# Weight splits moved around a step's events, with a shorter layer-norm chain and fp32 broadcasts, in a two-layer hybrid diffusion backbone

## The chip, the core and the metric

The kernel runs on one core of one Trainium2 chip. TensorE (PE in the rows, PEld for its weight loads) multiplies; VectorE (DVE), ScalarE (ACT) and GpSimd (POOL) do the element-wise work; SyncE (SP) issues the transfers. The metric is the device time of one execution in microseconds, lower is better.

## The reference

Two groups of tokens share the weights: 128 prompt tokens and 256 sample tokens of width 1024, so 384 columns in all. Each of two layers does

```
x <- LN(alpha*x + 0.5*gate1*SwiGLU_1(mod1(x)))
x <- LN(alpha*x + gate2*Mixer(mod2(x)))
x <- LN(alpha*x + 0.5*gate3*SwiGLU_2(mod3(x)))
```

where LN is a layer norm over the 1024 features, mod_i(x) = x*(1+scale_i)+shift_i with scale, shift and gate from a matrix `w_mod` times the conditioning vector, and SwiGLU goes through 2 x 2816 columns. The mixer has one input projection into queries, keys, values, a convolution branch (31 taps per channel), a pooling branch and three gates; differential attention over 4 heads; a projection of each branch, the gated sum of the three, and one output projection. Outputs are both groups' tokens, and keys and values of the prompt. All data is float32.

## The kernel before

Activations lie feature-major: `X` is 8 tiles of 128 features x 384 tokens. Every large matmul is done three times to keep float32 accuracy: weights and activations are split into a high part (`wh`, `xh`: a copy rounded to the matmul's reduced fp32) and a low part (`wl`, `xl`: the rest), and `mm3` adds wh·xh, wl·xh and wh·xl (lines 404, 405, 406) in one PSUM bank.

Weights come as 388 units of 128 x 1024, in the order of use. For each unit SP loads `raw` (8 buffers), ScalarE copies `wh <- raw` (`prep_h`, line 342), VectorE subtracts `wl <- raw - wh` (`prep_l`, line 351). Five buffers hold split units; more lie in the general slots while `extra` allows. One step is one call of `begin`: it makes sure that the units up to `self.lead` ahead are split, runs the step's events, and returns the unit on which TensorE then does 24 matmuls. `lead` starts at 2 behind each layer norm and grows by 1 a step to 5 (9 with `extra`). Events are closures due at a step: evacuations of PSUM banks, the stages of attention (`a`, `b_`, `c`, `d`: scores, softmax, transpose, product with V), the convolution's layer norm, the pooling chain (`low`, `pmm`). Behind the events come `after` work (`fold_tile`, lines 656 and 658), background work (`tap`, the convolution's taps, line 1096) and `mod_dve_step`, which does two multiply-and-sum instructions of 128 x 1024 (line 451) whenever `mod_acc`, raised by `mod_rate` a step, reaches 1. Each engine takes its instructions in the order in which this code issues them.

Six sub-layers s = 0 to 5 run; s = 1 and 4 are the mixers. Each ends in `ln_end`: sums of y and y² by matmuls with ones (`ln_stat`, line 543), a chain of small VectorE instructions on 128 x 3 numbers (lines 728 to 734 with `rsqrt`, three Newton steps), and a broadcast of 1/sigma and -mean/sigma over the partitions by matmuls (line 745). The next sub-layer's first four units are multiplied meanwhile with `X` not yet normalized (lines 699 to 702), and corrected later (`unfold`). The four units are split ahead of it: in the mixer by the steps of `w_out`, whose steps (`self.early`) run the events first and split behind them, copy and subtraction together.

Of the kernel before, what the change touches and what calls it, by code (L numbers as in the profile page):

```python
# [11 lines left out]
F32 = mybir.dt.float32  # L12
F32R = mybir.dt.float32r
BF16 = mybir.dt.bfloat16
I32 = mybir.dt.int32
AF = mybir.ActivationFunctionType
ALU = mybir.AluOpType
AX = mybir.AxisListType

D = 1024  # L20
# [82 lines left out]
NORM_AT = 3  # L103
EXTRA = 4
KIN = 2
RATES = (0.9, 0, 0.65, 0.65, 0, 0.3)

# [133 lines left out]
class Kernel:  # L243
# [5 lines left out]
    def __init__(self, tc, ctx, io):  # L249
        self.tc, self.nc, self.io = tc, tc.nc, io  # L250
        self.pool = ctx.enter_context(tc.tile_pool(name="sb", bufs=1))
        self.ps = ctx.enter_context(tc.tile_pool(name="ps", bufs=1, space=bass.MemoryType.PSUM))
        self.uid = 0
        self.early = False
        self.half = None
        self.cur = 0
        self.n_dma = 0
        self.n_prep = 0
        self.raw = {}
        self.w = {}  # L260
        self.events = []
        self.step = 0
        self.bg = deque()
        self.bg_rate = 0
        self.jobs_done = set()
        self.job_dma = deque()
        self.mv = {}
        self.mod_acc = 0.0
        self.mod_rate = 0.0
        q = [(0, j) for j in range(16, 24)]  # L270
        for i in range(1, 6):
            q += [(i, j) for j in range(24)]
        self.lead = self.NW
        self.extra = self.held = 0
        self.after = []
        self.after_rate = 2
        self.jobs = deque(q)
# [6 lines left out]
    def t(self, shape, dt=F32, name="k"):  # L284
        n = self.nm(name)
        return self.pool.tile(shape, dt, name=n, tag=n, bufs=1)
# [8 lines left out]
        return self.pool.tile([128, 432], F32, name=self.nm(name), tag="c", bufs=8)  # L295

    def tiny(self, n, dt=F32, name="y"):
        return self.pool.tile([128, 16], dt, name=self.nm(name), tag="tiny", bufs=24)[:, :n]

    def bank(self, name="mm"):  # L300
        return self.ps.tile([128, 512], F32, name=self.nm(name), tag="mm", bufs=6)
# [19 lines left out]
            self.n_dma += 1  # L321

    def prep(self, upto):
        while self.n_prep < min(upto, len(UNITS)):
            self.prep_h()
            self.prep_l()

    def prep_h(self):
        u = self.n_prep
        slots = sum(not isinstance(w[0], SlotUnit) for w in self.w.values()) >= self.NW - self.held  # L330
        self.n_prep += 1
        self.dma_w(u + 1)
        cols = UNITS[u][1]
        r = self.raw.pop(u)
        if slots:
            w = tuple(SlotUnit([self.slot(F32R, n) for _ in range(3)]) for n in ("wh", "wl"))
        else:
            w = tuple(self.pool.tile([128, 1024], F32R, name=self.nm(n), tag=n, bufs=self.NW) for n in ("wh", "wl"))
        step = NT if slots else cols
        cuts = [slice(a, min(a + step, cols)) for a in range(0, cols, step)]  # L340
        for c in cuts:
            self.nc.scalar.copy(w[0][:, c], r[:, c])  # L342
        self.w[u] = w
        self.half = (u, r, cuts)

    def prep_l(self):
        u, r, cuts = self.half
        self.half = None
        wh, wl = self.w[u]
        for c in cuts:  # L350
            self.nc.vector.tensor_sub(wl[:, c], r[:, c], wh[:, c].bitcast(F32))  # L351
# [20 lines left out]
    def begin(self, key, run=True):  # L372
        u = self.cur
        assert UNITS[u][0] == key, (UNITS[u][0], key)
        self.step += 1
        if self.early:
            self.run_events()
        self.prep(u + self.lead)
        self.run_events()
        self.lead = min(self.lead + 1, self.NW + self.extra)  # L380
        for _ in range(self.after_rate):
            self.run_after()
        self.dma_w(u + self.NW + self.WDMA)
        for _ in range(self.bg_rate):
            if self.bg:
                self.bg.popleft()()
        self.mod_acc += self.mod_rate
        while self.mod_acc >= 1.0:
            self.mod_acc -= 1.0
            self.mod_dve_step()  # L390
        self.cur += 1
        return self.w.pop(u)
# [268 lines left out]
    def unfold(self, p):  # L661
# [9 lines left out]
        nc.vector.tensor_add(z, z, T)  # L671
        return z

    def ln_end(self, b7, ab, keys):

        nc, st = self.nc, self.lns
# [45 lines left out]
        else:  # L722
            b = self.ln_stat(y7, sq)
            tot = self.tiny(6)
            nc.vector.tensor_add(tot, st["pre"], b[:, :6])
        ms, msq, v = self.tiny(3), self.tiny(3), self.tiny(3)
        rm, rh, rl = self.tiny(6), self.tiny(6, F32R), self.tiny(6, F32R)
        nc.vector.tensor_scalar(ms, tot[:, 0:3], 1.0 / D, None, ALU.mult)
        nc.vector.tensor_tensor(msq, ms, ms, ALU.mult)
        nc.vector.scalar_tensor_tensor(v, tot[:, 3:6], 1.0 / D, msq, ALU.mult, ALU.subtract)  # L730
        self.rsqrt(v, 3, out=rm[:, 0:3])
        nc.vector.scalar_tensor_tensor(rm[:, 3:6], ms, -1.0, rm[:, 0:3], ALU.mult, ALU.mult)
        nc.vector.tensor_copy(rh, rm)
        nc.vector.tensor_sub(rl, rm, rh.bitcast(F32))
        if keys:
            if self.half:
                self.prep_l()
# [1 line left out]
                self.run_after()  # L739
            main(ma, 3)  # L740
        R, M = self.sbank(), self.sbank()
        for o, B in ((0, R), (3, M)):
            for t in range(3):
                for n, x in enumerate((rh, rl)):
                    mm(B[:, 128 * t:128 * t + 128], x[:, o + t:o + t + 1].to_broadcast([128, 128]),
                       self.identr, start=n == 0, stop=n == 1)
        if keys:
            Rs = self.slot(name="R")
            nc.scalar.copy(Rs, R[:, :NT])
# [88 lines left out]
    def ffn(self, l, j, xs, outs, s, mod_rate):  # L838
        nc = self.nc
        self.mod_rate = mod_rate  # L840
        ah = [None] * NF

        def evac(f, g, u, folded=False):
            if folded:
                g, u = self.unfold(g), self.unfold(u)
            sl = self.slot(name="si")
            nc.scalar.activation(sl, g[:, :NT], AF.Silu)
            a = self.slot(name="a")
            nc.vector.tensor_mul(a, u[:, :NT], sl)  # L849

            def split():
                h, lo = self.slot(F32R, "ah"), self.slot(F32R, "al")
                nc.scalar.copy(h, a)  # L853
                nc.vector.tensor_sub(lo, a, h.bitcast(F32))
                ah[f] = (h, lo)
            self.at(1, split)

        if xs is None:
            outs = self.first_group(l, j)
            self.mod_acc = -1.0  # L860
            xs = self.first_xs
        self.ln_begin(s)
        fo = s > 0
        f0 = 3
        if fo:
            o2 = self.kouter([("ffn_in", l, j, 2), ("ffn_in", l, j, NF + 2)], xs, 8, KIN)
            self.at(1, lambda: evac(0, outs[0], outs[1], fo))
            self.at(2, lambda: evac(1, outs[2], outs[3], fo))
            self.at(2, lambda: evac(2, o2[0], o2[1]))
        else:  # L870
            for f in range(3):
                self.at(1, lambda f=f: evac(f, *outs[2 * f:2 * f + 2]))
        for f in range(f0, NF):
            bs = outs[6:] if f == 3 and not fo else []
            if f == 7:
                self.extra = 0
            for c in (f, NF + f)[len(bs):]:
                w = self.begin(("ffn_in", l, j, c))
                b = self.bank()
                self.mtile(b[:, :NT], w, xs)  # L880
                bs.append(b)
            self.at(1, lambda f=f, bs=bs: evac(f, *bs))
        del xs
        for m in range(8):
            b = None
            for q in range(3):
                w = self.begin(("ffn_out", l, j, m, q))
                if m == 0 and q == 2:
                    self.ln_gate()
                    self.ab = None if s == 5 else self.coef_ss(s + 1)  # L890
                if b is None:
                    b = self.bank()
                if m == 5 and q == 0:
                    self.mod_rate = 0
                self.mtile(b[:, :NT], w, ah, 8 * q, 8 if q < 2 else 6, q == 0, q == 2)
            if m < 7:
                self.at(1, lambda m=m, b=b: self.ln_evac(m, b))
        self.flush()
        return b


    def start(self):
# [7 lines left out]
        self.scT = self.scz[:, :, 0:2]  # L910
        self.sel = self.C[:, C_SEL:C_SEL + 2]
        self.ones = self.t([128, 1], name="ones")
        self.identr = self.t([128, 128], F32R, name="identr")
        self.ident = self.C[:, C_ID:C_ID + 128]
        nc.vector.memset(self.scz, 0.0)
        nc.vector.memset(self.ones, 1.0)
# [8 lines left out]
    def start_rest(self):  # L925
# [9 lines left out]
            nc.scalar.activation(self.scb[:, c, :], self.scb[:, c, :], AF.Silu)  # L935
        self.at(1, lambda: silu(0))
        self.at(1, lambda: silu(1))
        self.at(4, lambda: nc.vector.tensor_copy(self.identr, self.ident))

    def first_group(self, l, j):  # L940

# [93 lines left out]
    def mixer(self, l, xs, outs, s):  # L1035
# [572 lines left out]
        self.bg_rate = 0  # L1608
        self.ab = self.coef_ss(s + 1)
        outs = self.kouter([("w_out", l, m) for m in range(4)], mg)  # L1610
        self.early = True
        self.after_rate = 1
        self.extra = 0
        self.lead = 4
# [20 lines left out]
    def build(self):  # L1635
# [3 lines left out]
        for s in range(6):  # L1639
# [4 lines left out]
                b = self.ffn(l, i // 2, xs, outs, s, RATES[s])  # L1644
            xs = outs = None
            self.extra = 0
            self.early = False
            self.after_rate = 2
            xs, outs = self.ln_end(b, self.ab, self.first_keys(s + 1))

# [44 lines left out]
```

## Time and profile before

| | |
|---|---|
| median of 3 runs | 1755.76 us (1753.92 to 1758.45) |
| profiled execution | 1757.04 us |
| its span, first to last instruction | 1755.3 us |
| mean granted TensorE clock | 0.987 |
| busy: PE, DVE, ACT, POOL | 1706.0, 1303.9, 769.1, 305.4 us |

Matmuls are pipelined: one of 384 columns lasts 0.34 us and the next starts 0.175 us behind it. A wait is idle time of an engine, put down to the instruction whose end released it. A granted clock of 1.00 is 2.4 GHz, 0.50 is 1.2 GHz.

### The profile page before, as it was taken

Reading aid. Unit: us, or ns where it says so; the run is one execution under the profiler, and the core shown is the slowest. Engines: PE = TensorE matmul, PEld = TensorE weight load, DVE = VectorE, ACT = ScalarE, POOL = GpSimd, SP = SyncE. Lnnn points to the kernel's source line nnn. Section 1 sums busy time; section 2 is a strip of 40 time slices with the busy share of each in tenths; the row PEclk is TensorE's granted clock in tenths of the full one; section 3 lists DMA queues with packets and bytes.
Section 4 is the critical chain, followed back from the end, with each engine's and each line's share of the span. In section 5 each row is a group of like instructions: output and inputs, shape, how many; then the busy total and the mean of one; then the engine's idle time right before and its main releaser. Section 6 shows DMA issues by size and latency. Waiting matters only on the chain.

```text
span 1755.3 us, 26189 instructions
## 1 busy us (share of the span) xinstructions
PE 1706.0 (97%) x9734; PEld 1677.3 (96%) x9734; DVE 1303.9 (74%) x2268; ACT 769.1 (44%) x1377; POOL 305.4 (17%) x410
## 2 busy tenths in 40 slices
PE   7999999999999999999999999999899999999997
PEld 5999999998999999999999999999899999999997
DVE  3699997898868588878688787869996767753333
ACT  3523333755554383333364333347455436533332
POOL 0000023331313420001220000224222253000011
PEclk8999999999999999999999999999999999999998
DMA  9777766335434147666537666643444422654320
GB/s 364 255 230 227 234 219 210 121 106 161 136 110 143 60 143 231 213 199 207 185 109 217 206 209 195 217 132 119 140 126 115 145 76 84 196 162 117 121 75 36
DMA packets 86639, 287.45 MB, mean 164 GB/s; under 512 B 10096, under 2 KB 17520, under 8 KB 86512
## 3 DMA queue, kind: packets, MB, share of 16 engines
q1 hardware_dynamic: 86512, 285.79, 51.6%
q8 instruction: 76, 1.25, 0.3%
q14 instruction: 51, 0.42, 0.1%
HBM read 280.51 MB, written 2.62 MB: 161 GB/s over the span
## 4 chain that ended last, share of the span: by engine, by line
PE 79%; DVE 13%; ACT 4%; issue 3%; DMA 0%; SPq 0%; ACTq 0%; POOL 0%; DVEq 0%; POOLq 0%
PE mm L404 24%; PE mm L406 24%; PE mm L405 24%; DVE wl L351 4%; DVE acc L1096 2%; ACT wh L342 1%; PE mm L702 1%; PE mm L700 1%; PE mm L699 1%; PE mm L426 1%; PE mm L429 1%; PE mm L427 1%; PE tot L543 1%; PE m L959 0%; DVE hf L829 0%
## 5 line engine op out<-in xcount | busy, mean ns | idle before, releaser
L351 DVE TENSOR_TENSOR wl<-raw,wh 128x1024 fp32r<-128x1024 f32 (+3 forms) x438 | 480.3, 1113 | 319.9 <-ACT wh L342 308.7
L342 ACT CAST wh<-raw 128x1024 fp32r<-128x1024 f32 (+3 forms) x438 | 400.4, 934 | 613.5 <-issue 403.4
L404 PE MATMUL mm<-xh,wh 128*128 128x384 f32 x1796 | 611.8, 341 | 9.9 <-ACT e L1458 4.2
L405 PE MATMUL mm<-xh,wl 128*128 128x384 f32 x1796 | 608.5, 339 | 0.6 <-DVE wl L351 0.6
L406 PE MATMUL mm<-xl,wh 128*128 128x384 f32 x1796 | 608.5, 339 | 0.1
L404 PEld LDWEIGHTS mm<-xh,wh 128*128 128x128 f32 x1796 | 339.5, 189 | 15.4 <-ACT e L1458 4.6
L405 PEld LDWEIGHTS mm<-xh,wl 128*128 128x128 f32 x1796 | 339.6, 189 | 1.1 <-DVE wl L351 1.0
L406 PEld LDWEIGHTS mm<-xl,wh 128*128 128x128 f32 x1796 | 339.6, 189 | 0.4 <-DVE xl L833 0.4
L451 DVE SCALAR_TENSOR_TENSOR junk<-raw,scb 128x1024 bf16<-128x1024 f32 x256 | 312.4, 1220 | 4.5
L406 PE MATMUL mm<-al,wh 128*128 128x384 f32 x704 | 237.4, 337 | 0.0
L405 PE MATMUL mm<-ah,wl 128*128 128x384 f32 x704 | 237.3, 337 | 0.0
L404 PE MATMUL mm<-ah,wh 128*128 128x384 f32 x704 | 237.2, 337 | 0.0
L622 POOL TENSOR_SCALAR sq<-sq 128x384 f32<-128x384 f32 x6 | 7.0, 1173 | 784.9 <-ACT sq L619 784.9
L404 PEld LDWEIGHTS mm<-ah,wh 128*128 128x128 f32 x704 | 132.2, 188 | 0.0
L406 PEld LDWEIGHTS mm<-al,wh 128*128 128x128 f32 x704 | 132.2, 188 | 0.0
L405 PEld LDWEIGHTS mm<-ah,wl 128*128 128x128 f32 x704 | 132.2, 188 | 0.0
L1096 DVE SCALAR_TENSOR_TENSOR acc<-U,P,acc 128x399 f32<-128x399 f32 x120 | 85.7, 770 | 0.0
L619 ACT ACTIVATE sq<-X 128x384 f32<-128x384 f32 x42 | 22.1, 526 | 124.3 <-DVE X L608 123.3
L658 DVE SCALAR_TENSOR_TENSOR yl<-X,ab,yh 128x128 fp32r<-128x128 f32 x80 | 46.7, 608 | 24.9 <-ACT yh L656 24.6
L833 POOL TENSOR_TENSOR xl<-hf,xh 128x384 fp32r<-128x384 f32 x40 | 44.3, 1123 | 102.1 <-DVE t L771 83.6
L628 POOL TENSOR_TENSOR s<-s,X 128x384 f32<-128x384 f32 x30 | 30.6, 1019 | 170.2 <-DVE X L608 145.9
L853 ACT CAST ah<-a 128x384 fp32r<-128x384 f32 x88 | 44.3, 509 | 22.1 <-DVE a L849 22.1
(284 smaller groups left out, 2082.7 us busy)
## 6 DMA issues: line engine op xcount, KB each, us to landing
raw<-in_units SPq DMA_DIRECT2D x356, 512.0 KB, 3.8
raw<-in_wmod SPq DMA_DIRECT2D x144, 512.0 KB, 4.4
raw<-in_units SPq DMA_DIRECT2D x32, 384.0 KB, 3.7
X<-in_x SPq DMA_DIRECT2D x4, 384.0 KB, 7.1
K<-K SPq DMA_DIRECT2D x16, 96.0 KB, 5.0
out_y<-X SPq DMA_DIRECT2D x8, 192.0 KB, 2.0
scb<-in_cond SPq DMA_DIRECT2D x2, 512.0 KB, 8.2
Q<-QL SPq DMA_DIRECT2D x16, 64.0 KB, 4.7
```

What stands on the lines that cost most here:

```text
L342: self.nc.scalar.copy(w[0][:, c], r[:, c])
L351: self.nc.vector.tensor_sub(wl[:, c], r[:, c], wh[:, c].bitcast(F32))
L404: mm(out, wh, xh, start=first, stop=False)
L405: mm(out, wl, xh, start=False, stop=False)
L406: mm(out, wh, xl, start=False, stop=last)
L451: self.nc.vector.scalar_tensor_tensor(self.junk, r, 1.0, self.scb[:, c, :], ALU.mult, ALU.mult, accum_out=mv[:, j, c:c + 1])
L619: nc.scalar.activation(sq, x, AF.Square)
L628: nc.gpsimd.tensor_add(st["s1"], st["s1"], x)
L658: nc.vector.scalar_tensor_tensor(lo[:, a:b], x[:, a:b], self.ab[:, 0, m, c:c + 1], h[:, a:b].bitcast(F32), ALU.mult, ALU.subtract)
L833: (nc.gpsimd if pool else nc.vector).tensor_sub(xl, hf, xh.bitcast(F32))
L853: nc.scalar.copy(h, a)
L1096: nc.vector.scalar_tensor_tensor(acc[c][:, :399], U[c][:, j:j + 399], w, acc[c][:, :399], ALU.mult, ALU.add)
```

## The change

- `prep` is cut into `prep_cast` (all copies) and `prep_sub` (all subtractions); `half` becomes a list.
- `begin` issues copies, then events, then subtractions; while `lead` is under 4 the subtractions stay ahead of the events. `early` goes.
- `ln_scale` replaces the layer norm's chain: sums are used undivided, the first guess comes from one instruction, one Newton step and one step of third order follow. The fp32 broadcast `bcast` (line 536) replaces the pairs of high and low parts, so the copy `rh`, the subtraction `rl` and the rounded identity `identr` go.
- The modulation's rate in s = 2 and 3 goes from 0.65 to 0.7, and `mod_acc` starts each later SwiGLU at -2 steps' worth. `tiny` has 32 buffers in place of 24.

```diff
-RATES = (0.9, 0, 0.65, 0.65, 0, 0.3)
+RATES = (0.9, 0, 0.7, 0.7, 0, 0.3)
...
     def prep(self, upto):
+        self.prep_cast(upto)
+        self.prep_sub()
+
+    def prep_cast(self, upto):
         while self.n_prep < min(upto, len(UNITS)):
             self.prep_h()
+
+    def prep_sub(self):
+        while self.half:
             self.prep_l()
...
         self.step += 1
-        if self.early:
-            self.run_events()
-        self.prep(u + self.lead)
+        self.prep_cast(u + self.lead)
+        if self.lead < 4:
+            self.prep_sub()
         self.run_events()
+        self.prep_sub()
         self.lead = min(self.lead + 1, self.NW + self.extra)
...
+    def ln_scale(self, tot):
+        nc = self.nc
+        S, Q = tot[:, 0:3], tot[:, 3:6]
+        rm = self.tiny(6)
+        t = lambda dt=F32: self.tiny(3, dt, "rs")
+        nm, s2, v, i, h = t(), t(), t(), t(I32), t()
+        nc.vector.tensor_scalar(nm, S, -1.0 / D, None, ALU.mult)
+        nc.vector.tensor_tensor(s2, S, nm, ALU.mult)
+        nc.vector.tensor_tensor(v, Q, s2, ALU.add)
+        nc.vector.tensor_scalar(i, v.bitcast(I32), -0.5, float(0x5F3759DF), ALU.mult, ALU.add)
+        nc.vector.tensor_scalar(h, v, -0.5, None, ALU.mult)
+        y0 = i.bitcast(F32)
+        a, b, y, yd = t(), t(), t(), t()
+        nc.vector.tensor_tensor(a, y0, y0, ALU.mult)
+        nc.vector.tensor_tensor(b, a, h, ALU.mult)
+        nc.vector.scalar_tensor_tensor(y, b, 1.5, y0, ALU.add, ALU.mult)
+        a, b, u, w = t(), t(), t(), t()
+        nc.vector.tensor_tensor(a, y, y, ALU.mult)
+        nc.vector.tensor_scalar(yd, y, math.sqrt(D), None, ALU.mult)
+        nc.vector.scalar_tensor_tensor(b, a, -1.0, v, ALU.mult, ALU.mult)
+        c = math.sqrt(0.375)
+        nc.vector.tensor_scalar(u, b, 1.0, c, ALU.add, ALU.mult)
+        nc.vector.scalar_tensor_tensor(w, u, 0.5 / c, u, ALU.add, ALU.mult)
+        nc.vector.scalar_tensor_tensor(rm[:, 0:3], w, 1.0, yd, ALU.add, ALU.mult)
+        nc.vector.tensor_tensor(rm[:, 3:6], nm, rm[:, 0:3], ALU.mult)
+        return rm
...
-        ms, msq, v = self.tiny(3), self.tiny(3), self.tiny(3)
-        rm, rh, rl = self.tiny(6), self.tiny(6, F32R), self.tiny(6, F32R)
-        nc.vector.tensor_scalar(ms, tot[:, 0:3], 1.0 / D, None, ALU.mult)
-        nc.vector.tensor_tensor(msq, ms, ms, ALU.mult)
-        nc.vector.scalar_tensor_tensor(v, tot[:, 3:6], 1.0 / D, msq, ALU.mult, ALU.subtract)
-        self.rsqrt(v, 3, out=rm[:, 0:3])
-        nc.vector.scalar_tensor_tensor(rm[:, 3:6], ms, -1.0, rm[:, 0:3], ALU.mult, ALU.mult)
-        nc.vector.tensor_copy(rh, rm)
-        nc.vector.tensor_sub(rl, rm, rh.bitcast(F32))
+        rm = self.ln_scale(tot)
...
-        for o, B in ((0, R), (3, M)):
-            for t in range(3):
-                for n, x in enumerate((rh, rl)):
-                    mm(B[:, 128 * t:128 * t + 128], x[:, o + t:o + t + 1].to_broadcast([128, 128]),
-                       self.identr, start=n == 0, stop=n == 1)
+        self.bcast(R, rm[:, 0:3])
+        self.bcast(M, rm[:, 3:6])
...
         if fo:
+            self.mod_acc = -2 * mod_rate
+        if fo:
             o2 = self.kouter([("ffn_in", l, j, 2), ("ffn_in", l, j, NF + 2)], xs, 8, KIN)
...
-        self.at(4, lambda: nc.vector.tensor_copy(self.identr, self.ident))
```

## Rows read from the trace of the kernel before

**Rows 1.** The page: busy time and share of the span by engine.
```profile
PE 1706.0 (97%) x9734; PEld 1677.3 (96%) x9734; DVE 1303.9 (74%) x2268; ACT 769.1 (44%) x1377; POOL 305.4 (17%) x410
```
**Rows 2.** Waits of TensorE by releaser: us in total, times, longest us.
```profile
PE sm L745 <- DVE y L733: 6.5, 4, 3.5
...
PE sm L1483 <- ACT wT L1477: 5.3, 4, 2.0
PE mm L404 <- ACT e L1458: 4.2, 2, 2.1
...
PE mm L426 <- DVE t L1593: 3.0, 2, 1.5
PE mm L700 <- DVE wl L351: 2.4, 2, 1.2
PE sm L405 <- DVE wpl L1329: 2.2, 2, 1.1
...
PE mm L406 <- DVE ol L1521: 1.4, 2, 0.7
...
PE mm L405 <- DVE wl L351: 0.6, 1, 0.6
```
**Rows 3.** Stretches: length; PE, PEld, DVE, ACT, POOL busy; granted clock; DMA share; GB/s.
```profile
404.11:407.52 3.41, 3.41 (x13) 3.41 (x12) 2.38 (x6) 2.28 (x3) 0.00 (x0) 0.50 0.65 178
...
602.08:608.91 6.83, 6.83 (x26) 6.83 (x26) 5.87 (x27) 2.78 (x7) 0.00 (x0) 0.50 0.28 87
...
1322.30:1329.12 6.82, 6.52 (x19) 5.91 (x20) 6.39 (x12) 2.85 (x6) 5.88 (x11) 0.50 0.56 155
...
1458.83:1462.24 3.41, 3.41 (x12) 3.41 (x12) 2.99 (x16) 1.64 (x5) 0.00 (x0) 0.50 0.45 123
...
338.00:425.00 87.00, 82.86 (x445) 78.60 (x444) 81.18 (x143) 48.26 (x101) 25.66 (x41) 0.98 0.45 135
```
**Rows 4.** Layer-norm chain of s = 0 in time: start, us, engine, line [idle before].
```profile
315.66 0.16 DVE L728 TENSOR_SCALAR y<-tot 128x3 f32<-128x3 f32 x1 [1.03 <-PE tot L543]
...
316.45 0.17 DVE L516 TENSOR_SCALAR rsi<-rsi 128x3 int32<-128x3 int32 x1
316.53 0.16 DVE L518 TENSOR_SCALAR rsh<-y 128x3 f32<-128x3 f32 x1
316.65 0.16 DVE L522 TENSOR_TENSOR rsa<-rsi 128x3 f32<-128x3 f32 x1
...
318.61 0.17 DVE L733 CAST y<-y 128x6 fp32r<-128x6 f32 x1
...
318.84 1.64 PE L745 MATMUL sm<-identr,y 128*128 128x128 f32 x12 [1.00 <-DVE y L733]
```
**Rows 5.** TensorE in time: one fp32 broadcast of 3 columns, in s = 0.
```profile
90.40 0.83 PE L536 MATMUL sm<-C,y 128*128 128x128 f32 x6
```
**Rows 6.** ACT and DVE in time, in the last `w_out` step of s = 1.
```profile
596.70 1.03 ACT L342 CAST wh<-raw 128x1024 fp32r<-128x1024 f32 x1
...
597.76 1.62 DVE L351 TENSOR_TENSOR wl<-raw,wh 128x1024 fp32r<-128x1024 f32 x1 [1.59 <-ACT wh L342]
```
**Rows 7.** DVE in time at the end of the `ao` steps of s = 1.
```profile
560.53 2.19 DVE L351 TENSOR_TENSOR wl<-raw,wh 128x384 fp32r<-128x384 f32 x3 [1.05 <-ACT wh L342]
562.65 1.00 DVE L1593 SCALAR_TENSOR_TENSOR t<-ga,mm 128x384 f32<-128x384 f32 x2
```
**Rows 8.** DVE in time, in attention of s = 1.
```profile
400.36 1.21 DVE L351 TENSOR_TENSOR wl<-raw,wh 128x1024 fp32r<-128x1024 f32 x1
401.50 0.74 DVE L1453 TENSOR_REDUCE y<-mm 128x2 f32<-128x256 f32 x2
...
419.55 2.04 DVE L351 TENSOR_TENSOR wl<-raw,wh 128x1024 fp32r<-128x1024 f32 x1
```
**Rows 9.** DVE and PE in time, early in the mixer of s = 1.
```profile
352.13 2.35 DVE L351 TENSOR_TENSOR wl<-raw,wh 128x1024 fp32r<-128x1024 f32 x2
354.40 0.47 DVE L1204 SCALAR_TENSOR_TENSOR q<-mm,P,C 128x256 f32<-128x256 f32 x1
...
356.25 0.34 PE L404 MATMUL mm<-xh,wh 128*128 128x384 f32 x1
```

More of the change, by code (lines that the diff above doesn't have):

```diff
@@ L253, in __init__ @@
         self.uid = 0
-        self.early = False
-        self.half = None
+        self.half = []
         self.cur = 0
@@ L297, in tiny @@
     def tiny(self, n, dt=F32, name="y"):
-        return self.pool.tile([128, 16], dt, name=self.nm(name), tag="tiny", bufs=24)[:, :n]
+        return self.pool.tile([128, 16], dt, name=self.nm(name), tag="tiny", bufs=32)[:, :n]
     def bank(self, name="mm"):
@@ L343, in prep_h @@
         self.w[u] = w
-        self.half = (u, r, cuts)
+        self.half.append((u, r, cuts))
     def prep_l(self):
-        u, r, cuts = self.half
-        self.half = None
+        u, r, cuts = self.half.pop(0)
         wh, wl = self.w[u]
@@ L912, in start @@
         self.ones = self.t([128, 1], name="ones")
-        self.identr = self.t([128, 128], F32R, name="identr")
         self.ident = self.C[:, C_ID:C_ID + 128]
@@ L1610, in mixer @@
         outs = self.kouter([("w_out", l, m) for m in range(4)], mg)
-        self.early = True
         self.after_rate = 1
@@ L1646, in build @@
             self.extra = 0
-            self.early = False
             self.after_rate = 2
```

## The prediction

> **What bounds the kernel now.** I read the page first: TensorE is busy for 97% of the span [rows 1], so no other engine's saved work shows in the end time unless TensorE was waiting for it. Hence the second view, TensorE's waits, which is the list of what can be won. The reader should see in [rows 2] that almost every long one ends with VectorE: the layer-norm chain (L733), the weight subtraction (L351), or a small step of attention and merging that sits in VectorE's queue (the bank evacuations at L1593, `wpl`, `ol`) or one step behind it, on ScalarE (`e`, `wT`). Third, the granted clock by stretch. Five stretches between the start and the tail run at 0.50, that is 1.2 GHz; [rows 3] show four, and the fifth, at 468.97, is as long as the first. Together 3.41 + 3.41 + 6.83 + 6.82 + 3.41 = 23.9 us at half speed, so 11.9 us lost, each behind a stretch in which TensorE waited or ran one-column sums. Fourth, VectorE's timeline around each wait. There a subtraction stands in front of the instruction that TensorE wants, although it is for a unit several steps ahead.
>
> **The layer-norm chain.** From the first instruction to the start of the copy `rh` it takes 318.61 - 315.66 = 2.95 us, and the broadcast starts 0.23 us later, at 3.18 [rows 4]. Consecutive instructions that depend on each other start 0.20 us apart; the independent `rsh` starts 0.08 behind its neighbour, and what follows it 0.12 behind it [rows 4]. In the new order `nm, s2, v, i` take three gaps of 0.20, `h` fits between `i` and `a` (0.08 + 0.12), then `b, y, a` three gaps, `yd` fits in again (0.20), then `u, w` and `rm` three gaps: 0.6 + 0.2 + 0.6 + 0.2 + 0.6 = 2.2 us to the instruction that writes 1/sigma, plus the same 0.23: the broadcast at 2.4, so 0.78 us sooner. If it waits for -mean/sigma too, the gain is 0.58. It counts where TensorE stands waiting: four times, 6.5 us, of which 3.5 in the tail and about 1.0 behind each of s = 0, 2 and 3 [rows 2]. All four waits are longer than 0.78. **3.1 us** (2.3 to 3.1). In the mixers the chain ends under matmuls and the gain is nothing.
>
> The Trainium skill (VectorE: DVE Perf Modes, Rules for kernel authors) says not to fuse chained VectorE instructions for speed, since only their count matters. By count the chain goes from 17 to 14 before the broadcast, at 2.95/16 = 0.18 us each 0.55 us, and the term would be 2.2. The rows show that independent ones cost half, and they decide.
>
> **The fp32 broadcast.** Now 12 matmuls take 1.64 us [rows 4]. The trace has the replacement elsewhere: one fp32 broadcast of three columns leaves six records in 0.83 us [rows 5], so both together are twelve records in about 1.6. **0** (0.1 either way).
>
> The Trainium skill (FP8 and Floating Point Precision, TensorE Precision Notes) counts four passes for true fp32 and one read for the reduced form, so six fp32 matmuls would be 24 passes against 12. The row shows two records for each and no doubling, at 128 columns. It stays as a rival below.
>
> **Copies ahead, subtractions behind, in the `w_out` steps.** Before, events go first: the last copy starts at 596.70, in the queue behind a squaring which waits for VectorE's evacuation, and its subtraction at 597.76, after 1.59 us idle [rows 6]; TensorE, arriving at that unit, waits 1.2 us in each mixer [rows 2]. With the copy ahead of the events it needs only a free buffer, some 4 us (one step of 24 matmuls) earlier, and the subtraction follows one evacuation. **2.4 us** (1.2 to 2.4).
>
> **Events ahead of subtractions elsewhere.** Copies stay where they were on ScalarE, so only VectorE's order changes, by one subtraction per step.
> - The bank wait at L1593, 1.5 us in each mixer [rows 2]: a subtraction of 2.19 us, itself held 1.05 us by its copy, stands at 560.53 in front of the evacuation at 562.65 [rows 7]. Moved behind: **3.0** (0 to 3.0).
> - `ol`, 1.4 us in two [rows 2], the same picture with a subtraction of some 1.2 us in front: **1.4** (0 to 1.4).
> - `e`: the maximum at 401.50 stands behind a subtraction from 400.36 [rows 8]. 1.14 us off each of two waits of 2.1 [rows 2]: **2.3** (0 to 4.2).
> - `wT`: four waits, 5.3 us [rows 2]. The chain maximum, exponent, copy, `wT` starts behind subtractions of 1.2 to 2.04 us [rows 8], so the waits up to 1.2 go and of the longest, 2.0, some 0.8 may stay: **4.3** (2.0 to 5.3).
> - `wpl`, two waits of 1.1 [rows 2], one subtraction in front again, but the chain there has several links: **1.6** (0 to 2.2).
>
> **The clock.** Each of the five half-speed stretches follows waits that this change shortens; but one-column sums and transposes, which stay, fill part of the same time, and stretches may appear elsewhere. Between 0 and 11.9 us I take half: **6**.
>
> **Edits at nothing.** The raw buffer comes free one event group later, so SP issues a later transfer by the same; transfers are for units four steps (17 us) off. `fold_tile`, taps and modulation jobs, queued behind the subtraction, see the same sum of work before them. The rate of 0.7 adds about 1.3 jobs of 2 x 1.2 us to each of two SwiGLUs where VectorE is not full; the two steps' delay takes one job away from the stage's crowded start. The identity's copy and `tiny` lie off every wait. If these lost their cover, each costs at most one VectorE instruction, near 1 us. What is late next once the waits are gone: in the mixers' first third VectorE itself, busy 81.18 of 87 us [rows 3].
>
> **The sum.** 3.1 + 0 + 2.4 + 3.0 + 1.4 + 2.3 + 4.3 + 1.6 + 6 = 24.1 us. Against the profiled execution's 1757.04 that gives 1732.9; the median shown is 1.3 below that execution, so **1732 us**. All low ends: 2.3 + 1.2 + 2.0 = 5.5, 1750. All high ends: 3.1 + 2.4 + 3.0 + 1.4 + 4.2 + 5.3 + 2.2 + 11.9 = 33.5, 1722.
>
> **Rivals.**
> *VectorE stays the bound* (0.15). With 93% busy in 338 to 425 [rows 3], the maximum that comes a subtraction sooner is followed by the next thing late by as much, and the clock drops stay. Left are the chain, the `w_out` copies and the bank wait: 2.3 + 2.4 + 3.0 = 7.7, so 1748. Against it: the subtractions idle for their copies [rows 6, 7], idle time that the new order uses.
> *fp32 broadcasts at double price* (0.05): 1.64 us more in each of six layer norms [rows 4], 9.8 in all, 1742. Against it stand [rows 5].
> *The waits only change their names* (0.08): gains within a few us, e.g. the chain's 3.1 alone: 1753.
> *Weights late* (0.05), the one that ends slower. Place: the mixers' first dozen units, where the first of two subtractions from 352.13 ends near 353.3 and TensorE takes that unit at 356.25 [rows 9]: 2.9 us to spare. The events that now go ahead last 1.5 us there, up to the next group of taps; it decides once they, with what they wait for, exceed 2.9. Were each of 12 units in both mixers 1.4 us late, 34 us would be lost: 1766. For it: the subtraction now stands behind whatever the events wait for. Against it: L405 waits for `wl` once in the whole span, 0.6 us [rows 2], and while `lead` is under 4 the order stays.
> The Trainium skill (TensorE: Matmul & The Clock Gate, Architectural detail: the array is 16× 32×32) calls VectorE's queue strictly first-in first-out, which is what would make a subtraction wait with its event; the idle 1.59 us in front of one [rows 6] agrees.
>
> **How the numbers follow.** The forecast as summed has 0.67, with its own range of 1722 to 1742. Less than 0.3% (5.3 us) is about what runs of this kernel cannot tell from no change. Faster: 0.67 + 0.15 + 0.05 = 0.87; same 0.08; slower 0.05. The range from 1722 to 1749 takes in the first three cases but for their ends.
>
> **What would show it.** After: the wait of L745's successor near 0.2 to 0.4 in s = 0, 2, 3, and 2.7 in the tail; twelve fp32 records in 1.6 us; no wait of the layer norm's matmuls for `wl`; no bank wait at the output projection's start; `e` waits near 1.0; `wT` mostly gone; fewer stretches at 0.50. I am wrong if TensorE waits for `wl` in the steps between 345 and 400 us, if new waits of about the old length carry other names, or if the half-speed stretches stay or grow in number, which takes the 6 us away.

## The result, and the profile after

The changed kernel takes 1730.82 us (median of 4 runs, 1729.86 to 1732.49) against 1755.99 us before (4 runs, 1753.92 to 1758.45): a ratio of 0.9857, 95% interval 0.984 to 0.9874. The forecast was 1732 us, in a range of 1722 to 1749. The profiled execution of the changed kernel took 1732.49 us, 24.55 us less than that of before (the sum had 24.1).

Busy time by engine, from the page, and TensorE's waits (us in total, times, longest us), to be held against [rows 1, 2]. Lines have moved: 404, 405, 406 are now 410, 411, 412; the copy 348, the subtraction 356, the broadcast 542.

```profile
PE 1698.8 (98%) x9734; PEld 1673.3 (97%) x9734; DVE 1326.3 (77%) x2249; ACT 770.5 (45%) x1377; POOL 349.5 (20%) x410
```

```profile
PE mm L1472 <- POOL QL L1399: 7.0, 2, 3.5
...
PE sm L542 <- DVE y L705: 3.3, 4, 2.7
...
PE sm L410 <- ACT wT L1448: 1.3, 2, 0.7
```

Gone are the layer norm's wait for a weight's residue, the bank wait of the output projection, `ol`, `e` and `wT` at the prompt's value products (2.4 + 3.0 + 1.4 + 4.2 + 5.3 us before), and `wpl` (2.2). Two more went that the prediction's sum does not have, in the view of before:

```profile
PE mm L404 <- ACT PB L1260: 1.8, 2, 0.9
...
PE sm L404 <- DVE y L1133: 1.3, 2, 0.6
```

The chain's wait halved, 6.5 to 3.3. At the head stands a wait of 7.0 us that was not there: the scores of the first prompt task (L1472), once in each mixer. The view names GpSimd's `QL`. TensorE, VectorE and GpSimd in time:

```profile
388.50 0.61 PE L1472 MATMUL mm<-kp,qz 128*128 128x128 f32 x4
...
392.54 1.19 PE L1472 MATMUL mm<-kp,qz 128*128 128x128 f32 x4 [3.43 <-POOL QL L1399]
```

```profile
387.73 1.22 DVE L356 TENSOR_TENSOR wl<-raw,wh 128x1024 fp32r<-128x1024 f32 x1
388.87 2.26 DVE L1120 SCALAR_TENSOR_TENSOR acc<-U,P,acc 128x399 f32<-128x399 f32 x4
391.05 0.68 DVE L1210 SCALAR_TENSOR_TENSOR lam<-lam 128x1 f32<-128x1 f32 x1
391.65 0.74 DVE L1266 TENSOR_TENSOR vp<-mm,bv 128x256 f32<-128x256 f32 x2
```

```profile
390.79 1.72 POOL L1399 TENSOR_TENSOR QL<-q,Q 64x256 fp32r<-64x256 f32 x2 [10.57 <-ACT Q L1398]
```

TensorE resumes 0.15 us behind the end of `vp`, VectorE's evacuation of the first value bank, which stands behind a subtraction, four taps and a lambda instruction. It also resumes 0.03 us behind the end of `QL`, so these rows alone leave two candidates. The run without the guard (below) decides: there the same matmul starts 0.15 us behind `vp` again, while `QL` has only begun:

```profile
393.58 0.68 PE L1470 MATMUL mm<-kp,qz 128*128 128x128 f32 x4 [2.13 <-DVE vp L1264]
```

```profile
393.13 1.52 POOL L1397 TENSOR_TENSOR QL<-q,Q 64x256 fp32r<-64x256 f32 x2 [11.35 <-ACT Q L1396]
```

In all nine kernels with this wait, in both mixers, the matmul starts 0.15 us behind `vp`, wherever (in the first mixer between 388.87 and 393.43 us) that ends. Before, all eight score matmuls ran ahead of this evacuation, so the second tile lay in another of the six PSUM banks:

```profile
389.76 1.05 PE L1448 MATMUL mm<-kp,qz 128*128 128x128 f32 x8
```

```profile
393.08 0.74 DVE L1242 TENSOR_TENSOR vp<-mm,bv 128x256 f32<-128x256 f32 x2
```

The layer norm of s = 0, VectorE and then TensorE, against [rows 4]:

```profile
315.07 0.16 DVE L688 TENSOR_SCALAR rs<-tot 128x3 f32<-128x3 f32 x1 [0.99 <-PE tot L549]
...
317.25 0.16 DVE L705 SCALAR_TENSOR_TENSOR y<-rs,rs 128x3 f32<-128x3 f32 x1
```

```profile
317.46 1.60 PE L542 MATMUL sm<-C,y 128*128 128x128 f32 x12 [0.21 <-DVE y L705]
```

From the first instruction to the broadcast 317.46 - 315.07 = 2.39 us, where 2.4 was forecast; TensorE waits for `rm[:, 0:3]` alone, and the twelve fp32 records take 1.60 us against 1.64.

The clock by stretch, against [rows 3]:

```profile
391.36:398.19 6.83, 5.65 (x19) 5.68 (x20) 6.83 (x16) 0.82 (x2) 3.84 (x6) 0.50 0.56 173
...
1234.45:1241.28 6.83, 5.72 (x19) 5.75 (x20) 6.83 (x16) 0.65 (x2) 3.77 (x6) 0.50 0.71 244
...
338.00:425.00 87.00, 83.57 (x449) 79.82 (x448) 84.38 (x150) 49.61 (x103) 29.62 (x36) 0.96 0.44 131
```

With two more of 3.41 us, at 592.75 and 1435.84, half speed between start and tail makes 20.5 us, against 23.9. Both long stretches begin inside the new wait, so TensorE works for 18.2 us at half speed in place of 23.6. VectorE is busier than before in 338 to 425, 84.38 of 87 us.

By stage, after less before, from the first uses of the weight units: each of the layer norms of s = 0, 2 and 3 -0.9 and the tail -0.8; end of the mixer with its layer norm -3.5 and -2.0; pooling steps -3.65 and -4.9; `ol` and the output projection's bank together -2.4 in each mixer; attention only -1.3 and -1.4: in each mixer 2.9 to 3.0 us lost at the new wait and 4.2 to 4.4 won behind it.

### The profile page after: what moved, and what is told of

Its sections match the earlier page's. It is cut to its first block, busy times and chain, and to the rows that moved or that the text cites. A ratio compares the mean times of both kernels' runs of the same rounds, so it can differ in the third digit from the quotient of the medians.

```text
span 1730.5 us, 26092 instructions
## 1 busy us (share of the span) xinstructions
PE 1698.8 (98%) x9734; PEld 1673.3 (97%) x9734; DVE 1326.3 (77%) x2249; ACT 770.5 (45%) x1377; POOL 349.5 (20%) x410
## 4 chain that ended last, share of the span: by engine, by line
PE 95%; DVE 2%; ACT 1%; issue 1%; POOL 1%; DMA 0%; SPq 0%; ACTq 0%; DVEq 0%; POOLq 0%
PE mm L411 27%; PE mm L412 27%; PE mm L410 27%; PE mm L734 1%; PE mm L735 1%; PE mm L737 1%; PE mm L433 1%; PE mm L432 1%; PE mm L435 1%; PE sm L542 1%; PE tot L549 1%; PE mm L1260 1%; PE mm L1262 1%; PE mm L1261 1%; PE sm L1454 1%
## 5 line engine op out<-in xcount | busy, mean ns | idle before, releaser
L411 PE MATMUL mm<-xh,wl 128*128 128x384 f32 x1796 | 608.7, 339 | 0.7 <-DVE wl L356 0.7
L356 DVE TENSOR_TENSOR wl<-raw,wh 128x1024 fp32r<-128x1024 f32 (+3 forms) x438 | 485.3, 1124 | 106.2 <-ACT wh L348 100.9
L411 PEld LDWEIGHTS mm<-xh,wl 128*128 128x128 f32 x1796 | 339.2, 189 | 2.1 <-DVE wl L356 2.0
L411 PE MATMUL mm<-ah,wl 128*128 128x384 f32 x704 | 237.4, 337 | 0.0
L411 PEld LDWEIGHTS mm<-ah,wl 128*128 128x128 f32 x704 | 132.3, 188 | 0.0
L878 DVE TENSOR_TENSOR al<-a,ah 128x384 fp32r<-128x384 f32 x88 | 48.6, 557 | 81.3 <-ACT ah L877 78.5
L873 DVE TENSOR_TENSOR a<-mm,si 128x384 f32<-128x384 f32 x82 | 45.5, 556 | 75.9 <-ACT si L871 70.9
L1120 DVE SCALAR_TENSOR_TENSOR acc<-U,P,acc 128x399 f32<-128x399 f32 x120 | 81.1, 731 | 0.0
L634 POOL TENSOR_TENSOR s<-s,X 128x384 f32<-128x384 f32 x30 | 42.4, 1412 | 151.9 <-DVE X L614 129.2
L664 DVE SCALAR_TENSOR_TENSOR yl<-X,ab,yh 128x128 fp32r<-128x128 f32 x80 | 67.6, 882 | 6.2 <-ACT yh L662 6.0
```

The costliest lines, as they stand in the source:

```text
L411: mm(out, wl, xh, start=False, stop=False)
L634: nc.gpsimd.tensor_add(st["s1"], st["s1"], x)
L664: nc.vector.scalar_tensor_tensor(lo[:, a:b], x[:, a:b], self.ab[:, 0, m, c:c + 1], h[:, a:b].bitcast(F32), ALU.mult, ALU.subtract)
L1120: nc.vector.scalar_tensor_tensor(acc[c][:, :399], U[c][:, j:j + 399], w, acc[c][:, :399], ALU.mult, ALU.add)
```

## Experiments

All times are medians; ratios are to the kernel before, run on the same chip beside them (1755.66 to 1757.03 us). These medians of one kernel are up to 1.4 us apart, so a difference to the changed kernel below that tells nothing. Each edit is to the changed kernel unless it says otherwise.

**The chain and the broadcast alone**, put into the kernel before:

```diff
+        rm = self.ln_scale(tot)
...
+        self.bcast(R, rm[:, 0:3])
+        self.bcast(M, rm[:, 3:6])
```

> The kernel before with the new layer-norm chain and the fp32 broadcast alone. If the prediction's term is right: the wait for the chain falls by 0.8 us at s = 0, 2, 3 and in the tail, 3.1 to 3.6 us in all, about 1752.5. If fp32 broadcasts cost double (rival): 9.8 us back, about 1762. If the chain was hidden anyway: 1756.

1754.81 us (10 runs, 1751.66 to 1757.30), ratio 0.9993 (0.9983 to 1.0002): no difference that can be told. The waits did as expected:

```profile
PE sm L536 <- DVE y L699: 3.3, 4, 2.7
```

Three of the ten runs lie at 1751.7 to 1752.1 us with a mean granted clock of 0.991, the others at 1754 to 1757 with 0.987 to 0.990; the kernel before runs at 0.986 to 0.988 and 1754.4 to 1757.6. The run that was profiled is one of the three. Its waits are 3.2 us shorter, and between start and tail it has 17.1 us of half speed against 23.9, although one stretch had grown, where [rows 3] have 3.41 us at 1458.83:

```profile
1451.29:1458.11 6.82, 6.82 (x26) 6.82 (x26) 5.88 (x25) 2.74 (x7) 0.00 (x0) 0.50 0.26 82
```

The seven longer runs were not profiled. That they win the 3.2 us at the waits too, and lose them to the clock, is argued and not shown.

**The new order alone**, with the old chain, the pairs and the old pacing (the lines are against the kernel before):

```diff
-        if self.early:
-            self.run_events()
-        self.prep(u + self.lead)
+        self.prep_cast(u + self.lead)
+        if self.lead < 4:
+            self.prep_sub()
         self.run_events()
+        self.prep_sub()
```

> The changed kernel with the old chain, the paired broadcast and the old modulation rates, so the new order of copies, events and subtractions alone. If the gains add up: 1730.8 + 3.5 = 1734, with the new wait of 3.4 us in front of the prompt's second score bank in both mixers. If chain and order overlap (the rival: one hides behind the other): 1737 or more.

1734.40 us, ratio 0.9873 (0.9856 to 0.9889). The order is worth 21 of the 25 us. The changed kernel, which has the new chain, broadcast and pacing besides, is 3.6 us faster still, so the gains add up as the theory had it. The order also brings the new wait, and a fifth wait for the old chain, 0.69 us at the end of the first mixer, where the prediction had put the chain at nothing:

```profile
PE sm L780 <- DVE y L768: 7.2, 5, 3.5
PE mm L1483 <- POOL QL L1410: 6.9, 2, 3.5
```

**Subtractions ahead of the events, as the copies:**

```diff
-        if self.lead < 4:
-            self.prep_sub()
+        self.prep_sub()
```

> The changed kernel with the subtractions always in front of the events; copies stay ahead of both. If a subtraction in VectorE's queue is what held attention and merging: the gains left are the chain (3.5) and the w_out steps with their clock (5.5), about 1747; the bank wait at the output projection (1.5 each), ol (0.7 each) and the e waits (2.1 each) come back, and the new 3.4 us wait is gone. If what the events won is taken back by the new wait (rival): 1731 to 1736.

1741.58 us, ratio 0.9923 (0.9907 to 0.9938), 10.8 us more than the changed kernel: less than the theory's loss, more than the rival's. Six of the waits of before (`wT`, `e`, the output projection's bank, `wpl`, `PB`, `ol`) are back to about a tenth of a microsecond, and the new one is gone:

```profile
PE sm L1506 <- ACT wT L1500: 5.3, 4, 2.0
...
PE mm L409 <- ACT e L1481: 4.3, 2, 2.2
...
PE mm L431 <- DVE t L1616: 2.9, 2, 1.5
```

At the end of the mixers it gains, against the kernel before, 5.1 and 3.5 us, more than the changed kernel, since no half-speed stretch is left there.

**Copies behind the events too**, where four or more units are split ahead:

```diff
-        self.prep_cast(u + self.lead)
-        if self.lead < 4:
-            self.prep_sub()
+        ahead = self.lead < 4
+        if ahead:
+            self.prep(u + self.lead)
         self.run_events()
-        self.prep_sub()
+        if not ahead:
+            self.prep(u + self.lead)
```

> The changed kernel, but where four or more units are split ahead, a step's copies on ScalarE stand behind the step's events too, ahead of the subtractions. Theory (the waits at the output projection of the mixer went because the weights' copies no longer wait behind the layer norm's evacuation): the waits of 1.2 us at the norm's weight residue come back, in each mixer, and with them up to a half-speed stretch each: 1733 to 1738 us. Rival (only the place of the subtractions matters, copies have room): 1730.8 us within 1.5.

1767.84 us, ratio 1.0058 (1.0043 to 1.0073): 37 us more than the changed kernel and slower than before. The waits at the norm came back as the theory had it, with 10.24 us of half speed behind:

```profile
602.69 0.45 PE L735 MATMUL mm<-yh,wh 128*128 128x388 f32 x1 [0.52 <-ACT wh L348]
604.34 0.44 PE L736 MATMUL mm<-yh,wl 128*128 128x388 f32 x1 [1.20 <-DVE wl L356]
```

That is 5.5 us in each mixer. What both theories missed is attention, 13.5 us in each mixer. ScalarE, VectorE and TensorE in time:

```profile
410.01 0.37 ACT L1483 ACTIVATE e<-mm,y 128x128 f32<-128x128 f32 x1 [6.27 <-DVE y L1479]
...
411.86 1.06 ACT L348 CAST wh<-raw 128x1024 fp32r<-128x1024 f32 x1
```

```profile
409.74 0.17 DVE L1479 TENSOR_SCALAR y<-y 128x4 f32<-128x4 f32 x1
412.95 1.23 DVE L356 TENSOR_TENSOR wl<-raw,wh 128x1024 fp32r<-128x1024 f32 x1 [3.03 <-ACT wh L348]
414.09 2.20 DVE L1121 SCALAR_TENSOR_TENSOR acc<-U,P,acc 128x399 f32<-128x399 f32 x3
```

```profile
413.24 0.71 PE L1508 MATMUL sm<-vp,wT 128*128 128x128 f32 x4 [2.37 <-ACT wT L1502]
```

The copy is queued behind the exponentials, these wait for VectorE's maximum, the subtraction waits for the copy, and the taps and the next softmax step queue behind the subtraction: VectorE stands still for 3.03 us in the stretch where it has nothing to spare. The costliest groups of the page count this idle time, as the last two fields (us, and the part that ended with the copy); the changed kernel first, this one second:

```profile
L356 DVE TENSOR_TENSOR wl<-raw,wh 128x1024 fp32r<-128x1024 f32 (+3 forms) x438 | 485.3, 1124 | 106.2 <-ACT wh L348 100.9
```

```profile
L356 DVE TENSOR_TENSOR wl<-raw,wh 128x1024 fp32r<-128x1024 f32 (+3 forms) x438 | 493.8, 1144 | 272.8 <-ACT wh L348 259.1
```

The same field is 319.9 us before and 306.2 with subtractions ahead. So it is neither the early copy nor the late subtraction that frees VectorE, but the events between them.

**The guard `lead < 4` taken out:**

```diff
-        if self.lead < 4:
-            self.prep_sub()
```

> The changed kernel, but subtractions stand behind a step's events always, also while fewer than four units are split ahead. Theory: at the starts of the stages the split weights come 1 to 3 us before TensorE needs them, and a step's events there take VectorE 2 to 3 us, so that the guard is worth up to 1.5 us in each of the few steps with both: 1731 to 1736 us, with new waits of TensorE for a weight's residue at the starts of stages. Rival (the guard does nothing here, the weights have room): 1730.8 us within 1.5.

1738.18 us, ratio 0.9898 (0.9883 to 0.9913): 7.4 us more, above the theory's range. The weight's residue is late in seven places, one of them at the kernel's start as in the changed kernel,

```profile
PE mm L409 <- DVE wl L356: 9.5, 7, 2.8
```

up to 2.8 us at the start of the second SwiGLU of either layer, where the subtraction stands behind the correction of the norm. It is late by 1.2 us once in each mixer too, at 348.97 and 1193.52, among the first units, where the prediction's rival "weights late" stood. The guard keeps that rival out.

**The modulation's old pacing** (0.65 and no delayed start):

```diff
-RATES = (0.9, 0, 0.7, 0.7, 0, 0.3)
+RATES = (0.9, 0, 0.65, 0.65, 0, 0.3)
...
-        if fo:
-            self.mod_acc = -2 * mod_rate
```

> The changed kernel with the modulation's old pacing (0.65 a step in the feed-forward, no delayed start). Theory (that work is off every wait that sets TensorE's time): 1731 us within 1.5. Rival (the pacing was worth something at the start of the feed-forward, where VectorE is busiest): 1733 to 1737 us, with waits for a weight's residue there.

1731.97 us, ratio 0.986 (0.9846 to 0.9875): the same. TensorE's waits for a weight's residue at L411 are 1.6 us in two, in place of 0.7 in one, so the new pacing saves a wait of 0.8 us, less than the runs can tell.

**The pairs back in the broadcast**, with the new chain:

```diff
+        rh, rl = self.tiny(6, F32R), self.tiny(6, F32R)
+        nc.vector.tensor_copy(rh, rm)
+        nc.vector.tensor_sub(rl, rm, rh.bitcast(F32))
...
-        self.bcast(R, rm[:, 0:3])
-        self.bcast(M, rm[:, 3:6])
+        for o, B in ((0, R), (3, M)):
+            for t in range(3):
+                for n, x in enumerate((rh, rl)):
+                    mm(B[:, 128 * t:128 * t + 128], x[:, o + t:o + t + 1].to_broadcast([128, 128]),
+                       self.identr, start=n == 0, stop=n == 1)
```

> The changed kernel, but the two rows of the layer norm are again split into high and low halves, and broadcast by twelve fp32r matmuls instead of six fp32 ones. Theory: two VectorE instructions of 0.20 us each come back on the chain, 0.4 us at each of the five norms, 2.0 us, and the broadcast itself takes as long as before: 1732.8 us (1731 to 1734), the wait at the norm's product 0.4 us longer each. Rival (the fp32 broadcast cost more than the pairs, or the clock takes the difference): 1729 to 1731 us.

1731.56 us, ratio 0.9858 (0.9842 to 0.9875). The four waits are 0.4 us longer each, as expected,

```profile
PE sm L775 <- DVE y L763: 4.9, 4, 3.1
```

but the time can't be told from the changed kernel's.

**Fewer taps in the value and first-score steps**, to free the value evacuation:

```diff
-BG = (4, 4, 3, 3, 2)
+BG = (4, 2, 3, 3, 2)
```

> The changed kernel with 2 convolution taps a step in place of 4 in the four value steps, so 8 taps (4.5 us of VectorE) move behind the value evacuation. If the new wait is for a PSUM bank that VectorE's value evacuation frees late, behind the taps: the wait of 3.4 us in each mixer falls under 0.5 and the two half-speed stretches behind it (6.8 us each, 3.4 us lost each) go, so 7 to 14 us less, 1717 to 1724. If it is a wait for GpSimd's QL, as the table of waits names it (rival): unchanged, 1731.

1728.15 us, ratio 0.9841 (0.9827 to 0.9856), an interval that overlaps the changed kernel's. The evacuation now starts at 386.04 us, the wait at L1472 and the half speed behind it are gone, and the stages up to there gain some 6 us in each mixer, as they should if the wait was for VectorE's evacuation. But the convolution's own norm begins later and is not done at its projection. There the code runs the events of the steps still missing at once (the loop on `conv_hl`), with no matmuls between them, and TensorE waits for an attention step among them:

```profile
PE sm L1454 <- ACT wT L1448: 7.8, 2, 3.9
```

with 6.83 us of half speed behind it: the stage behind the pooling steps grows by 8.6 us in the first mixer.

**No taps in the fourth value step alone, five in each of the two steps behind it:**

```diff
         for i in range(4):
+            if i == 3:
+                self.bg_rate = 0
...
-BG = (4, 4, 3, 3, 2)
+BG = (4, 4, 5, 3, 2)
```

> The changed kernel, but no convolution tap is issued in the step of the fourth value unit, and five instead of three in each of the two pool-input steps behind it: the same taps, four of them moved behind the value evacuation. TensorE's order of instructions is that of the changed kernel, apart from which PSUM bank a score tile gets. Theory 1 (the second score bank of the first prompt task waits for VectorE's value evacuation, which stands behind taps): the wait of 3.5 us goes, and with it the half-speed stretch of 6.83 us behind it, which is worth at most half its length, 3.4 us; in both mixers. Slowing all the taps took 6 us out of that stage in each mixer against the changed kernel, so 1730.8 - 12 = 1719 us (1716 to 1723), and no new wait at the value product, since the convolution's chain starts where it does in the changed kernel. Rival (VectorE has no room: five taps of 1.13 us in a step of 4.2 us push subtractions and attention back): a wait of 1 to 4 us elsewhere in each mixer, 1724 to 1731 us.

1730.27 us, ratio 0.9851 (0.9836 to 0.9866): the same as the changed kernel. (A tap takes 0.57 us, not the 1.13 of the expectation.) The profile now names the evacuation itself, at 0.7 us, and the next in line takes the time:

```profile
PE mm L410 <- ACT e L1484: 5.7, 2, 2.9
...
PE mm L1474 <- DVE vp L1268: 1.5, 2, 0.8
```

**The same pause, with four taps a step in attention, or three and never made up for** (`BG` of 4, 4, 3, 4, 2 and of 4, 4, 3, 3, 2):

> The changed kernel without taps in the step of the fourth value unit; three taps in each of the two pool-input steps, as in the changed kernel, and four instead of three in each attention step, which makes up for the four left out. In the kernel with five taps in the pool-input steps the score bank's wait fell from 3.5 to 0.7 us, but the maxima of the first prompt task came at 400.9 us and TensorE waited 2.9 us for the bank of its exponentials. Here four taps fewer, 2.2 us, stand ahead of those maxima. Theory (that second wait is made by the taps alone): it falls to 0.7 us or less, and 2.8 us and about 3 us of half speed are won in each mixer: 1730.3 - 10 = 1720 us (1717 to 1725). Rival (VectorE has no room in this stretch at all: what is put off meets the attention's later steps): the wait moves to a later softmax or to the product with the values, 1726 to 1732 us.

> As the kernel with four taps in each attention step, but three there: the four taps left out in the step of the fourth value unit are never made up for, so the convolution's chain begins about one and a half steps later, where slowing all the taps began it nearly three steps later and had TensorE wait 3.9 us for the transposed weights in each mixer. Theory (that wait came from the place of the chain): 1718 to 1722 us if this place does not collide. Rival (it collides as there): a wait of 1 to 4 us at the value product in each mixer, 1724 to 1730 us.

1736.08 us, ratio 0.9878 (0.9861 to 0.9894), and 1735.19 us, ratio 0.9876 (0.9862 to 0.9891). Both medians lie 4 to 5 us above the changed kernel's and no run of theirs is as short as its longest, though the intervals overlap. Both rivals hold, and worse than they said. `e` waits 0.7 us in either; with four taps a step attention waits instead, with three the convolution is late for its projection, as with fewer taps:

```profile
PE sm L1509 <- ACT wT L1503: 5.0, 3, 2.1
PE sm L410 <- ACT wT L1450: 3.9, 2, 2.3
```

```profile
PE mm L410 <- ACT ch L1181: 4.6, 2, 2.3
PE mm L412 <- DVE cl L1187: 3.6, 2, 1.8
```

**Four of the 31 taps on GpSimd**: eight taps less for VectorE in each mixer and four additions more. The pacing of the first stages changes with it, and the clearing of `PB` moves to the mixer's start (not shown):

```diff
-BG = (4, 4, 3, 3, 2)
+BG = (4, 3, 2, 3, 2)
...
+        def g_mul(c, j, dst):
+            for lo, hi, g in SEGS:
+                o = lo + 15 * g + j
+                nc.gpsimd.tensor_scalar(dst[:, lo:hi], U[c][:, o:o + hi - lo], self.par(("dw", l, c), 1, j), None, ALU.mult)
...
+            nc.gpsimd.tensor_add(gacc[c], gacc[c], gt[0])
...
-            for j in range(KC):
+            for j in range(KC - GT):
```

> The changed kernel with the last four of the 31 convolution taps of each channel block on GpSimd (16 multiplications of a part each and 6 sums in a mixer, between its rotary work and the attention's residues), joined to VectorE's sum by four additions; the pacing of the first stage is 3 and 2 taps a step in place of 4 and 3, so that the convolution's chain starts at the same of TensorE's instructions. Eight taps of 0.56 us leave VectorE, and 1.3 us of additions come: 3.2 us less in each mixer. Theory (VectorE has no room from the value units to the first softmax, so that moving taps only moves the wait, and taking work off it removes it): the score bank's wait falls from 3.5 us to under 1 us, no wait over 1 us takes its place, the half-speed stretch behind it goes: 1719 us (1716 to 1724). Rival (GpSimd's 17 us or so delay the attention's residues, or slow VectorE's taps beside it): TensorE waits 1 to 5 us for those in each mixer, 1727 to 1740 us.

1734.45 us, ratio 0.9873 (0.9857 to 0.989), 3.6 us above the changed kernel with intervals that overlap; the rival holds. The score bank's wait stayed (now under its own name), and `wT` joined it:

```profile
PE mm L1510 <- DVE vp L1309: 7.0, 2, 3.5
PE sm L1545 <- ACT wT L1539: 5.1, 2, 2.8
```

VectorE was not relieved, because the price of a tap rose. First the changed kernel's group, then this one's:

```profile
L1120 DVE SCALAR_TENSOR_TENSOR acc<-U,P,acc 128x399 f32<-128x399 f32 x120 | 81.1, 731 | 0.0
```

```profile
L1126 DVE SCALAR_TENSOR_TENSOR acc<-U,P,acc 128x399 f32<-128x399 f32 x104 | 84.7, 867 | 0.0
```

Sixteen fewer taps cost 3.6 us more. This run tells nothing about a VectorE with less to do, since it had more: 1333.4 us busy against 1326.3.

## Why the prediction was right

The mechanism was right: the order of copies, events and subtractions, taken alone, gives 21 of the 25 us, and the three other orders that were run cost 7 to 37 more. That the total came out to half a microsecond is luck. TensorE's waits over 0.15 us, without those of the start, were 29.1 us in total and are 11.6: 17.5 us net, against 18.1 in the sum's terms. But 24.5 us went, 3.1 of them in waits that the sum does not have (`PB` and `y`), and the new wait put 7.0 back. The clock gave 2.7 us where 6 was taken. The rest, some 4.3 us, no term has; an estimate for 2.8 of it is that each of 17 waits fewer also saves the overlap of two matmuls, 0.34 - 0.175 = 0.17 us, which the view does not count. Some 1.5 us stay open. By term:

- *Chain, 3.1:* right in size and place; 0.79 us at each of the four waits, 3.5 by stage. Taken out of the changed kernel with the broadcast and the pacing it costs 3.6 us; alone in the kernel before it does not show in the median.
- *fp32 broadcast, 0:* right, 1.60 us; with the pairs back nothing but the 0.4 us on the chain changes.
- *Copies in the `w_out` steps, 2.4:* right in mechanism, shown by taking it out, and the 2.4 us are gone; with the half speed behind the waits it is worth 5.5 us a mixer there.
- *Bank wait at the output projection 3.0 and `ol` 1.4:* together 4.9 us measured, all gone.
- *`wpl`, 1.6:* with the clock behind it the pooling steps gave 8.6 us.
- *`e` and `wT`, 2.3 + 4.3:* this step failed. The old waits went, 4.2 and 5.3 us, more than forecast; but attention gave 2.7 us net. What was written of a rival, "the maximum that comes a subtraction sooner is followed by the next thing late by as much", is what happened at one place: the score tile that now waits for `vp`. The nine kernels with this wait show its cause. Why the tile got another bank is not settled; it did in every kernel with events ahead of subtractions but for the one with copies behind as well, and the one with fewer taps does not tell, since its evacuation ends before the matmul comes.
- *Clock, 6:* mis-sized. TensorE works for 5.4 us less at half speed, worth half of that, 2.7. Some 6.8 us were won where waits went, 5.1 of them in the pooling steps, and the two new stretches, less the one that they replace in attention, took 4.0 of it back.
- *Edits at nothing:* right for pacing. The guard, which the prediction names only against "weights late", holds 7.4 us.

Of the prediction's signs of being wrong one came: a wait as long as the longest of the old ones, under another name, in each mixer. Half-speed stretches went from five to four, where "fewer" was forecast.

Of the rivals, "VectorE stays the bound" is half true. It held from the value steps to the end of the convolution: four ways of moving taps and one of giving them away moved the wait to `e`, `wT`, `ch` or back, and none beat the changed kernel by more than its intervals. That the bound is VectorE's total work there is argued from these and from 84.38 busy of 87 us; a run with less work on VectorE was not had.

## What to carry to other kernels

If an in-order engine waits for another's result and has independent work, issue the producer first, that work between, and the consumer last: putting both ahead or both behind cost 11 and 37 us here. Where few units are ready ahead, keep the consumer in front of that work: the guard is worth 7.4 us. Read a gain from a wait list only after asking what the same engine does next; where it is busy 97% of a stretch, waits change their names. The engine named as releaser can be wrong when one instruction waits for several: here `QL` ended closer to TensorE's start than `vp`, which it waited for. Move one candidate and see whether the wait follows.

## What was not expected of the hardware

A tap (VectorE, two tensor operands in SBUF) slows while GpSimd works beside it. Three taps, first in the changed kernel with GpSimd idle, then with GpSimd adding taps from 378 us on:

```profile
398.44 1.71 DVE L1120 SCALAR_TENSOR_TENSOR acc<-U,P,acc 128x399 f32<-128x399 f32 x3
```

```profile
384.22 2.82 DVE L1126 SCALAR_TENSOR_TENSOR acc<-U,P,acc 128x399 f32<-128x399 f32 x3
```

0.57 against 0.94 us for one. The Trainium skill (SBUF — State Buffer, SBUF: two separate sides) says that a VectorE instruction with two SBUF inputs and a GpSimd instruction that reads SBUF shut each other out for a whole instruction. The trace agrees for GpSimd's instructions on two tensors. The lambda instruction, one column with two SBUF operands, takes 0.15 us with GpSimd idle (first row, the run with a pause in the fourth value step); in the changed kernel it takes 0.68 us beside the first `QL` (second row; `lam` from 391.05 is shown above) and ends 0.02 us behind it, as a lock would have it and a shared rate would not:

```profile
388.62 0.15 DVE L1210 SCALAR_TENSOR_TENSOR lam<-lam 128x1 f32<-128x1 f32 x1
```

```profile
390.79 0.92 POOL L1399 TENSOR_TENSOR QL<-q,Q 64x256 fp32r<-64x256 f32 x1 [10.57 <-ACT Q L1398]
```

So it is in eight runs, twice in each, and 0.53 us of the new wait come from it: `lam` stands ahead of `vp`. Beside GpSimd's products with a scalar the rows do not show a lock of a whole instruction: a tap from 390.05 to 390.89 ended inside one from 389.92 to 390.91 (GpSimd's spans are rough).

The granted clock, too, was less steady than expected: ten runs of one kernel had means of 0.987 to 0.991 and times 5.6 us apart, as much as the smallest edits here are worth.
